# Casts, differences and sums held in the text's order, and background loads begun a turn earlier, in a hybrid HGRN2/GLA decoder trunk

## The chip, the cores and the metric

The kernel runs on one core of one Trainium2 chip, as one launch. The metric is the device time of that launch in microseconds (us); smaller is better. The core has a matmul engine (TensorE, PE in the profile; its weight loads are PEld), VectorE (DVE), ScalarE (ACT), GpSimd (POOL) and SyncE (SP). Each engine works off its own queue in order and waits on semaphores for the others. DMA transfers are issued here from SP's queue (loads) and POOL's queue (mostly stores).

## What is computed

The reference is one layer of a conditioned decoder trunk on a sequence of 1024 positions with 1024 channels, in float32. The normalised and modulated input `h` goes through one wide projection `w_in`; its columns feed eight HGRN2 heads and four GLA heads, gates and merge gates. Cut to what matters:

```python
h = rms_norm(x, norm_w) * (1 + scale) + shift
hq, hf, hi, hz, gq, gk, gv, gz, ga, mg = split(h @ w_in)
# HGRN2: f = lb + (1-lb)*sigmoid(hf); log_f = log f; k = (1-lb)*sigmoid(-hf); q = silu(hq); v = hi
# GLA:   log_a = log_sigmoid(ga @ alpha_w + alpha_b) / 16;  q, k, v = gq, gk, gv
# each head, in chunks of 64:  S_t = diag(decay_t) S_{t-1} + k_t v_t^T,  o_t = S_t^T q_t
y_h = rms_norm(o_hgrn) * silu(hz);  y_g = rms_norm(o_gla) * silu(gz)
u_h, u_g = y_h @ w_branch[0], y_g @ w_branch[1]
merged = sigmoid(mg[0]) * u_h + sigmoid(mg[1]) * u_g
out = rms_norm(x + gate * (merged @ w_out), final_norm_w)
```

## The kernel before

**Matmuls in three passes.** Every large product is done in a faster float format (fp32r): an operand is split into a high part, which is a cast on ACT (L202 in `split`, L208 in `pinned_split`), and a low part, the operand minus the high part, on DVE (L203, L209). PE then adds three products: high by high, high by low, low by high. So before PE can use a loaded weight block, a load, a cast on ACT and a subtraction on DVE must have been done.

**Jobs.** Matmul work is a list of jobs that the class `Stream` goes through. A job `Feat` projects 128 features of one head (L591: 8 steps, called units here, of 6 matmuls, into a PSUM tile `pd`). A job `Vjob` is a part of the value projections (L1864), which are done as two-by-two block products with seven instead of eight products (the Strassen-Winograd scheme); these need differences of blocks of `h` (`make_factor`, L1703, stored to memory as `fx`) and sums of blocks of the weights (`v_sums`, L1718 to L1724, stored as `vs`; L1824 to L1828 in `Vjob.prep` for the first value projection). The job list is: the value projection of the GLA heads, the projections of the GLA heads, the value projection of the HGRN heads, and the three projections of each of the eight HGRN heads. The later stages (merge gates, both branch projections, output) use the same scheme (L1315), and their weight sums are made in advance in `weight_sums` and stored as `ws`.

**What sets the order.** The Python text issues all instructions in one sequence. `Stream.ahead` issues the loads (`load_feat`, L573) and splits (`split_feat`) of later jobs while a job runs. After each unit `weave` lets two side tracks advance: `side`, where a head's attention runs beside the projections of the next (`attention`, L641 to L816), and `back`, the background: `alpha_side` (the decays of the last two GLA heads, L920 to L939), then `v_sums`, then `prepare`, which calls `weight_sums` for 16 blocks, then `gate_side`. Only the first generator of a track runs. Each `yield n` says how many units of the main stream are to pass before the generator goes on, and the number in `stream.back.append` how many to wait at the start.

Over this text lies the framework's scheduler. It keeps dependences, but may place an instruction on its engine's queue ahead of those that stand before it in the text, or behind them, by its own estimate of when inputs are ready and by priorities. `tc.keep_in_program_order` takes an instruction out of that: it keeps the text's place on its engine. Before, it is used only for the casts in `pinned_split`. The sums of `weight_sums` have a lowered priority (`BEHIND = -400`), by which they fill gaps.

**Attention of a head**, as far as it matters: ACT and DVE scale q and k (L641 to L654), PE makes scores in several block sizes (L649, L680, L738 to L749) with evictions between them, DVE masks the last ones (L753), ACT copies the score blocks into the tile `scT` (L758, L761 and the four of L764), PE transposes k (L775), ACT evicts that (L776), and PE makes the chunk states (L795) and then the outputs (L814, L816). For an HGRN head the gates are made just before from a projection: L1070 and L1071 on ACT, L1072 to L1074 on DVE.

**Memory.** Nearly all tiles are one of 46 slots of 4 KB per partition. A slot that is used again makes its new writer wait for the last reader, and for a store out of it.

## Time and profile before

| | us |
|---|---|
| median of 3 runs (lowest to highest) | 1217.03 (1217.02 to 1219.02) |
| profiled execution, own time | 1218.36 |
| its span, first to last instruction | 1216.7 |
| mean granted PE clock | 0.988 |

PE is busy for 96% of the span, DVE for 70%, ACT for 48%, POOL for 10%; the DMA engines move 181 GB/s on the mean. The profile names an instruction by its line, the engine, the operation and the tiles (output <- inputs; `b` is any slot). A number in square brackets behind a row is the idle time of its engine just before it, and what ended it. Busy time of PE is modelled, so idle time of PE that ends with a named release is the safer number. The granted clock is what the throttle let PE have, with 1.00 for full speed.

### The profile page before, as it was taken

The numbers are of one execution on the slowest core, as the hardware profiler recorded it, in microseconds if no ns is written. First come the engines' busy times: TensorE is split into PE (matmuls) and PEld (weight loads), VectorE is DVE, ScalarE is ACT, GpSimd is POOL, SyncE is SP. The second block draws the span as 40 slices with busy tenths as digits, with TensorE's granted clock in tenths as the row PEclk, the third lists the DMA queues.
The fourth block names the chain that finished last, engine by engine and source line by source line (L and its number), as shares of the span: only waits on it lengthen the run. The fifth ranks groups of instructions, "written<-read, shape, count | busy, mean of one in ns | idle before, by whom it ended". The sixth has DMA issues, their size and how long they took to land.

```text
span 1216.7 us, 20300 instructions
## 1 busy us (share of the span) xinstructions
PE 1173.9 (96%) x8137; PEld 956.0 (79%) x8137; DVE 846.7 (70%) x1270; ACT 584.0 (48%) x859; POOL 122.9 (10%) x256
## 2 busy tenths in 40 slices
PE   7998999999999999899998999999999999999997
PEld 6775777788878788688886888878878888878886
DVE  4746567668565966777875896786454765988994
ACT  5674365643353744244234245356644544544554
POOL 4211101011100123011111000000020000000000
PEclk9998999999999999899998999999999999999999
DMA  9756336384644669345545542245697846435433
GB/s 325 258 212 227 111 121 191 114 283 140 225 129 166 226 225 327 106 147 192 173 155 160 165 119 79 83 140 162 219 325 278 265 157 212 147 104 173 160 102 137
DMA packets 150353, 220.19 MB, mean 181 GB/s; under 512 B 8939, under 2 KB 107297, under 8 KB 150258
## 3 DMA queue, kind: packets, MB, share of 16 engines
q1 hardware_dynamic: 131970, 157.84, 41.6%
q0 software_dynamic: 18240, 61.04, 13.1%
q8 instruction: 64, 1.05, 0.4%
q14 instruction: 31, 0.25, 0.1%
q10 hardware_dynamic: 48, 0.01, 0.0%
HBM read 153.84 MB, written 65.01 MB: 180 GB/s over the span
## 4 chain that ended last, share of the span: by engine, by line
PE 48%; issue 35%; DMA 5%; DVE 4%; POOL 4%; ACT 2%; SPq 1%; POOLq 0%; DVEq 0%; ACTq 0%
PE pd L1315 10%; PE pd L591 8%; PE pd L1864 8%; PE pm L1315 5%; PE sc_ps L1315 5%; PE pd L1492 3%; DMA b<-in_ada_w_dram 2%; POOL ws L1173 2%; PE pd L383 2%; PE sc_ps L1492 2%; PE pm L1492 1%; DVE b L209 1%; PE pm L814 1%; PE sc_ps L383 1%; PE pm L816 1%
## 5 line engine op out<-in xcount | busy, mean ns | idle before, releaser
L591 PE MATMUL pd<-b,b 128*128 128x512 f32 x1632 | 393.8, 397 | 0.0
L591 PEld LDWEIGHTS pd<-b,b 128*128 128x128 f32 x1632 | 304.8, 190 | 65.2 <-issue 0.7
L1315 PE MATMUL pd<-b,b 128*128 128x512 f32 x720 | 173.0, 391 | 1.5 <-DVE b L1302 1.0
L1864 PE MATMUL pd<-b,b 128*128 128x512 f32 x672 | 164.1, 398 | 3.0 <-ACT b L1747 1.7
L1315 PEld LDWEIGHTS pd<-b,b 128*128 128x128 f32 x720 | 134.0, 188 | 31.8 <-DVE b L1302 1.5
L1864 PEld LDWEIGHTS pd<-b,b 128*128 128x128 f32 x672 | 123.8, 188 | 36.9 <-ACT b L1747 4.9
L1258 DVE TENSOR_TENSOR b<-b,b 128x1024 fp32r<-128x1024 f32 x56 | 68.3, 1223 | 69.8 <-ACT b L1257 56.9
L202 ACT CAST b<-b 128x1024 fp32r<-128x1024 f32 (+1 forms) x70 | 65.9, 951 | 80.0 <-DMA b<-in_w_in_dram 22.9
L203 DVE TENSOR_TENSOR b<-b,b 128x1024 fp32r<-128x1024 f32 (+1 forms) x70 | 76.7, 1101 | 36.7 <-ACT b L202 35.8
L1257 ACT CAST b<-b 128x1024 fp32r<-128x1024 f32 x56 | 58.4, 1049 | 66.3 <-PE pm L1315 17.6
L1315 PE MATMUL sc_ps<-b,b 128*128 128x512 f32 x324 | 78.7, 391 | 0.6 <-ACT b L1287 0.6
L209 DVE TENSOR_TENSOR b<-b,b 128x1024 fp32r<-128x1024 f32 x44 | 52.7, 1225 | 35.8 <-ACT b L208 34.2
L1315 PE MATMUL pm<-b,b 128*128 128x512 f32 x300 | 72.1, 389 | 0.0
L1315 PEld LDWEIGHTS sc_ps<-b,b 128*128 128x128 f32 x324 | 60.5, 188 | 14.1 <-ACT b L1287 1.3
L1235 DVE TENSOR_TENSOR b<-b,b 128x1024 fp32r<-128x1024 f32 x48 | 57.8, 1222 | 19.7 <-ACT b L1234 13.9
L1234 ACT CAST b<-b 128x1024 fp32r<-128x1024 f32 x48 | 49.7, 1049 | 44.9 <-PE pd L1315 15.5
L1315 PEld LDWEIGHTS pm<-b,b 128*128 128x128 f32 x300 | 56.3, 188 | 11.7
L700 ACT COPY xb<-b 128x512 f32<-128x512 f32 x48 | 29.2, 619 | 62.4 <-PE sc_ps L680 36.4
L383 PE MATMUL pd<-b,b 128*128 128x512 f32 x192 | 52.8, 408 | 6.0 <-DVE b L359 5.2
L1173 POOL DMA_DIRECT2D ws<-b x64 | 34.5, 540 | 187.2 <-DVE b L1167 67.1
L383 PEld LDWEIGHTS pd<-b,b 128*128 128x128 f32 x192 | 34.8, 190 | 18.7 <-DVE b L359 6.1
L208 ACT CAST b<-b 128x1024 fp32r<-128x1024 f32 x44 | 44.3, 1050 | 6.8 <-PE pd L1864 3.5
(315 smaller groups left out, 1720.1 us busy)
## 6 DMA issues: line engine op xcount, KB each, us to landing
b<-in_w_in_dram SPq DMA_DIRECT2D x72, 512.0 KB, 4.9
ws<-b POOLq DMA_DIRECT2D x64, 256.0 KB, 4.4
b<-ws SPq DMA_DIRECT2D x32, 512.0 KB, 4.3
b<-in_x_dram SPq DMA_DIRECT2D x16, 512.0 KB, 6.2
b<-in_ada_w_dram SPq DMA_DIRECT2D x32, 256.0 KB, 6.5
v<-b POOLq DMA_DIRECT2D x32, 256.0 KB, 3.1
b<-v SPq DMA_DIRECT2D x16, 512.0 KB, 5.0
b<-fx SPq DMA_DIRECT2D x16, 512.0 KB, 4.2
```

What stands on the lines that cost most here:

```text
L202: nc.scalar.copy(hi, src)
L203: nc.vector.tensor_sub(lo, src, hi.bitcast(F32))
L209: nc.vector.tensor_sub(lo, src, hi.bitcast(F32))
L383: nc.tensor.matmul(accs[f], wg(a, d, f), b[d][:, half * 512:half * 512 + 512], start=(d == 0 and n == 0), stop=(d == KT - 1 and n == 2))
L591: nc.tensor.matmul(ps[0:w, th * 512:(th + 1) * 512], a[:, k, 0:w], b[:, th * 512:(th + 1) * 512], start=(k == 0 and n == 0), stop=(k == KT ...
L1173: nc.gpsimd.dma_start(w_sums[b][i // 2][q][:, i % 2 * 512:i % 2 * 512 + 512], parts[p].rearrange("p k f -> p (k f)"))
L1235: nc.vector.tensor_sub(lo, src, hi.bitcast(F32))
L1257: nc.scalar.copy(hi, t)
L1258: nc.vector.tensor_sub(lo, t, hi.bitcast(F32))
L1315: nc.tensor.matmul(o, a[:, sl], c, start=(p in (1, 5) and kt == 0 and n == 0), stop=(kt == 3 and n == 2), skip_group_check=True)
L1492: nc.tensor.matmul(o, a, b, start=(p in (1, 5) and kt == 0 and n == 0), stop=(kt == 3 and n == 2), skip_group_check=True)
L1864: nc.tensor.matmul(st.bank[i], x_, w_, start=(p in (1, 5) and kk == 0 and a == 0 and n == 0), stop=(kk == 1 and a == 1 and n == 2), skip_g ...
```

## The change

Five edits, all of them about order and time of issue; the arithmetic is the same.

- `split_feat` uses `pinned_split`, so the casts of all projection weights are held in the text's order on ACT.
- Held on DVE: the subtractions of `make_factor`, the sums of the value weights in `Vjob.prep` and `v_sums`, and the sums of `weight_sums`, which lose their lowered priority.
- `prepare` issues the loads of block n before the sums of block n − 1, so that a block's loads are a whole turn ahead of its sums; the waits between steps and the slot threshold (12 to 11) are adapted. In `v_sums` the wait between loads and sums is 9 units, not 6.
- In `attention` the four copies L764 move behind the eviction L776 of the transposed k.
- `alpha_side` for the last two GLA heads starts after 72 units, not 62.

```diff
-    def pinned_split(src):
-        hi, lo = S.get([2, 512], F32R), S.get([2, 512], F32R)
-        tc.keep_in_program_order(nc.scalar.copy(hi, src))
+    held = tc.keep_in_program_order
+
+    def pinned_split(src, hi=None, lo=None):
+        if hi is None:
+            hi, lo = (S.get(list(src.shape[1:]), F32R) for _ in range(2))
+        held(nc.scalar.copy(hi, src))
         nc.vector.tensor_sub(lo, src, hi.bitcast(F32))
         return hi, lo
...
-        split(raw[:, :, 0:w], hi[:, :, 0:w], lo[:, :, 0:w])
+        pinned_split(raw[:, :, 0:w], hi[:, :, 0:w], lo[:, :, 0:w])
...
-        for j in range(4):
-            nc.scalar.copy(scT[32 * j:32 * j + 32, :, 32 * j:32 * j + 32], blk[32 * j:32 * j + 32])
         scoring.discard(me)
         yield 3
...
         S.free(k)
+        for j in range(4):
+            nc.scalar.copy(scT[32 * j:32 * j + 32, :, 32 * j:32 * j + 32], blk[32 * j:32 * j + 32])
         yield 2.5
...
-    def weight_sums(b, i):
+    def load_blocks(b, i):
         src = sources[b][i]
-        while len(S.free_list) < 12 or paused[0]:
-            yield 1
-        x1, x2 = S.get([4, 2, P]), S.get([4, 2, P])
...
-        yield 6
+        return x
+
+    def weight_sums(b, i, x1, x2):
...
-        with tc.high_priority(offset=BEHIND):
-            add(parts[7], x1[:, :, 0], x1[:, :, 1])
-            add(parts[5], x1[:, :, 1], x2[:, :, 1])
-        yield 1.5
-        with tc.high_priority(offset=BEHIND):
-            add(parts[6], parts[7], x2[:, :, 1])
-            add(parts[3], parts[6], x2[:, :, 0])
+        held(add(parts[7], x1[:, :, 0], x1[:, :, 1]))
+        yield 1
+        held(add(parts[5], x1[:, :, 1], x2[:, :, 1]))
+        yield 1
+        held(add(parts[6], parts[7], x2[:, :, 1]))
+        yield 1
+        held(add(parts[3], parts[6], x2[:, :, 0]))
...
     def prepare():
-        for b in range(4):
-            for i in range(4):
-                yield from weight_sums(b, i)
+        todo = [(b, i) for b in range(4) for i in range(4)]
+        blocks_of = {}
+        for n in range(len(todo) + 1):
+            while n < len(todo) and (len(S.free_list) < 11 or paused[0]):
+                yield 1
+            if n < len(todo):
+                blocks_of[n] = load_blocks(*todo[n])
+            if n:
+                yield from weight_sums(*todo[n - 1], *blocks_of.pop(n - 1))
+            yield 7
...
-        nc.vector.tensor_sub(xq[dst][kk], xq[x][kk], xq[y][kk])
+        held(nc.vector.tensor_sub(xq[dst][kk], xq[x][kk], xq[y][kk]))
...
-            yield 6
+            yield 9
...
-                add(wq[0, 0][kk], wq[0, 0][kk], wq[0, 1][kk])
-                add(wq[0, 1][kk], wq[0, 1][kk], wq[1, 1][kk])
+                held(add(wq[0, 0][kk], wq[0, 0][kk], wq[0, 1][kk]))
+                held(add(wq[0, 1][kk], wq[0, 1][kk], wq[1, 1][kk]))
...
-        stream.back.append([alpha_side((2, 3)), 62, 1, 0])
+        stream.back.append([alpha_side((2, 3)), 72, 1, 0])
```

The order on the engines is shown at three places. Line numbers of the changed kernel are a little higher: L202/L203 and L208/L209 are both L211/L212 there, L641 to L657 are 3 higher, L764 is L780, L776 is L777, L900 to L1074 are 3 higher, L1703 is L1712.

Place 1, DVE's queue before the first GLA head (near 100 us). L1703/L1712 are the subtractions of `make_factor`, L900 to L906 (L903 to L909) the chain of the first decays, L359/L362 an eviction of q and k projections. Before:

```order
L203 TENSOR_TENSOR b_154<-b_973,b_146 128x512
L1703 TENSOR_TENSOR b_630<-b_630,b_915 128x1024
L1703 TENSOR_TENSOR b_834<-b_834,b_973 128x1024
L1703 TENSOR_TENSOR b_915<-b_915,b_1124 128x1024
L1703 TENSOR_TENSOR b_973<-b_973,b_1125 128x1024
L900 TENSOR_SCALAR b_1046<-b_1045 128x1024
L901 SCALAR_TENSOR_TENSOR b_1045<-b_1046,b_1045 128x1024
L906 TENSOR_TENSOR b_1046<-b_1046,b_1045 128x1024
L209 TENSOR_TENSOR b_1076<-b_1031,b_1075 128x1024
L359 TENSOR_SCALAR b_1089<-pd_173 128x512
```

Now:

```order
L203 TENSOR_TENSOR b_154<-b_973,b_146 128x512
L903 TENSOR_SCALAR b_1046<-b_1045 128x1024
L904 SCALAR_TENSOR_TENSOR b_1045<-b_1046,b_1045 128x1024
L909 TENSOR_TENSOR b_1046<-b_1046,b_1045 128x1024
L212 TENSOR_TENSOR b_1076<-b_1031,b_1075 128x1024
L362 TENSOR_SCALAR b_1089<-pd_173 128x512
L364 COPY b_1115<-sc_ps 128x512
L362 TENSOR_SCALAR b_1095<-pd_173 128x512
L212 TENSOR_TENSOR b_1165<-b_1035,b_1164 128x1024
L364 COPY b_1121<-sc_ps 128x512
L362 TENSOR_SCALAR b_1101<-pd_174 128x512
L1712 TENSOR_TENSOR b_1125<-b_834,b_1125 128x1024
```

The subtractions of `make_factor` left the stretch ahead of the decay chain and stand behind the third eviction; the second L212 now stands ahead of that one.

Place 3, ACT's queue at the first HGRN head (near 480 us). L641/L644 starts the scaling of q, L1070/L1073 and L1071/L1074 make the gates of the head, L202/L211 are casts of projection weights. Before:

```order
L946 ACTIVATE b_4065<-pd_3962 128x1024
L641 COPY xb<-b_4065 128x32x32
L202 CAST b_4486<-b_4263 128x1024
L202 CAST b_4609<-b_4385 128x1024
L1070 ACTIVATE b_4139<-pd_4068 128x1024
L1071 ACTIVATE b_4140<-pd_4068 128x1024
```

Now, and behind it DVE's queue at the same head (L1075 to L1077 are the gates on DVE, L1168 to L1174 sums of `weight_sums`, L645 to L648 the scaling that ends before PE's first scores):

```order
L949 ACTIVATE b_4031<-pd_3934 128x1024
L211 CAST b_4069<-b_3818 128x1024
L644 COPY xb<-b_4031 128x32x32
L1073 ACTIVATE b_4101<-pd_4034 128x1024
L1074 ACTIVATE b_4102<-pd_4034 128x1024
L211 CAST b_4144<-b_3856 128x1024
```

```order
L1077 TENSOR_SCALAR b_4102<-b_4102,oml 128x1024
L1168 TENSOR_TENSOR b_4122<-b_4015 128x512
L1170 TENSOR_TENSOR b_4121<-b_4015,b_4016 128x512
L1172 TENSOR_TENSOR b_4121<-b_4122,b_4016 128x512
L212 TENSOR_TENSOR b_4145<-b_3856,b_4144 128x1024
L1174 TENSOR_TENSOR b_4122<-b_4121,b_4016 128x512
L645 TENSOR_TENSOR xb<-b_4031,b_4101 128x32x8
L646 TENSOR_TENSOR xb<-b_4031,b_4101 128x32x8x2
L654 TENSOR_TENSOR b_4031<-b_4031,b_4101 128x256
L647 TENSOR_TENSOR xb<-xb,b_4101 128x32x16
L648 TENSOR_TENSOR xb<-xb,b_4101 128x32x8
```

On ACT no cast stands between L644 and L1073 any more; on DVE four sums and a subtraction stand between L1077 and L645.

Place 4, ACT's queue at a later HGRN head (near 654 us). L758/L761, L761/L764 and L764/L780 copy score blocks, L776/L777 evicts the transposed k. Before:

```order
L946 ACTIVATE b_5700<-pd_5579 128x1024
L202 CAST b_6370<-b_6138 128x1024
L202 CAST b_6245<-b_6022 128x1024
L641 COPY xb<-b_5700 128x32x32
L758 COPY scT<-sc_ps 32x4x32 x4
L761 COPY scT<-sc_ps 64x4x64 x2
L764 COPY scT<-blk 32x8x32 x4
L776 COPY b_5804<-pm_5805 128x512
```

Now:

```order
L949 ACTIVATE b_5672<-pd_5551 128x1024
L644 COPY xb<-b_5672 128x32x32
L761 COPY scT<-sc_ps 32x4x32 x4
L764 COPY scT<-sc_ps 64x4x64 x2
L211 CAST b_5775<-b_5549 128x1024
L777 COPY b_5779<-pm_5780 128x512
L777 COPY b_5779<-pm_5786 128x384
L780 COPY scT<-blk 32x8x32 x4
```

The two casts left the place ahead of L641; another cast, for the next job, stands ahead of the evictions of the transposed k, and the four copies stand behind them.

More of the change, by code (lines that the diff above doesn't have):

```diff
@@ L27 @@
 N_SLOTS = 46
-EVICT_FIRST, BEHIND = 300, -400
+EVICT_FIRST = 300
 PACE, PACE_H = 1.08, 1.15
@@ L1151, in hybrid_trunk_kernel @@
     paused = [False]
-    def weight_sums(b, i):
+    def load_blocks(b, i):
         src = sources[b][i]
-        while len(S.free_list) < 12 or paused[0]:
-            yield 1
-        x1, x2 = S.get([4, 2, P]), S.get([4, 2, P])
-        for kh, x in enumerate((x1, x2)):
-            nc.sync.dma_start(x.rearrange("p k a f -> p k (a f)"),
+        x = [S.get([4, 2, P]) for _ in range(2)]
+        for kh in range(2):
+            nc.sync.dma_start(x[kh].rearrange("p k a f -> p k (a f)"),
                               src[kh * 512:(kh + 1) * 512, :].rearrange("(k p) f -> p k f", p=P))
-        yield 6
+        return x
+    def weight_sums(b, i, x1, x2):
         s1, s2 = S.get([2, 4, P]), S.get([2, 4, P])
```

11 lines of the change are left out of this document (5 added, 6 removed).

## The prediction

> **What bounds the kernel now.** I read the busy shares first, then TensorE's (PE's) waits, then the granted clock in stretches of 20 us, and last the timelines of the long stalls. From the page, the engine row and the group of the weight casts (busy and mean ns, idle before it):
>
> ```profile
> PE 1173.9 (96%) x8137; PEld 956.0 (79%) x8137; DVE 846.7 (70%) x1270; ACT 584.0 (48%) x859; POOL 122.9 (10%) x256
> ```
>
> ```profile
> L202 ACT CAST b<-b 128x1024 fp32r<-128x1024 f32 (+1 forms) x70 | 65.9, 951 | 80.0 <-DMA b<-in_w_in_dram 22.9
> ```
>
> Matmuls bound the kernel, and no work is taken from PE, so the change can only win what PE idles or runs at a lower clock. ACT is half idle, but 80.0 us of its idle time stand in front of one line, the cast of a projection weight; where such a cast is early in ACT's queue and its data late, all behind it waits. PE's own waits (total, times, longest):
>
> ```profile
> PE pm L795 <- ACT b L776: 9.2, 5, 5.2
> PE pd L383 <- DVE b L359: 5.2, 1, 5.2
> PE sc_ps L649 <- DVE xb L645: 4.8, 1, 4.8
> PE pm L775 <- ACT b L922: 2.7, 1, 2.7
> PE pd L1864 <- ACT b L1747: 1.7, 4, 1.1
> ```
>
> Four single stalls make 17.9 us (5.2, 5.2, 4.8, 2.7), and four more before L795 share 9.2 − 5.2 = 4.0. The stretches (columns PE, PEld, DVE, ACT, POOL busy, granted clock, DMA share, GB/s) show a second price:
>
> ```profile
> 100.00:120.00 20.00, 14.77 (x51) 10.66 (x50) 10.87 (x12) 8.95 (x10) 3.27 (x7) 0.83 0.61 241
> 220.00:240.00 20.00, 19.14 (x96) 16.56 (x97) 10.58 (x16) 13.97 (x15) 0.00 (x0) 0.91 0.28 84
> 460.00:480.00 20.00, 20.00 (x89) 16.52 (x88) 12.71 (x22) 10.36 (x10) 5.20 (x10) 1.00 1.03 333
> 480.00:500.00 20.00, 15.19 (x114) 12.38 (x113) 16.41 (x26) 5.23 (x7) 3.42 (x7) 0.84 0.61 209
> 520.00:540.00 20.00, 19.13 (x106) 16.28 (x105) 16.02 (x28) 10.54 (x19) 2.69 (x5) 1.00 0.57 173
> 640.00:660.00 20.00, 14.94 (x174) 11.95 (x172) 10.45 (x19) 10.21 (x19) 2.16 (x4) 0.94 0.52 155
> 660.00:680.00 20.00, 19.83 (x126) 17.26 (x130) 15.40 (x26) 3.63 (x6) 2.70 (x5) 0.89 0.64 203
> ```
>
> The clock is full where PE is never idle (460) and where it idles for 0.9 us (520, one of the small L795 waits), and drops after each of the four long stalls: 20 × (1 − 0.83) = 3.4 us lost, then 1.8, 3.2, and 20 × (0.06 + 0.11) = 3.4: 11.8 us together. The four stalls thus cost about 30 us, and everything hangs on what holds them.
>
> **The change, place by place.** It adds and removes no instruction (DVE has 1235 rows in the order before and after); it moves them, so each term is a stall that goes or comes.
>
> *Place 1, about 107 us: subtractions held behind L359.*
>
> ```profile
> 99.53 0.69 ACT L898 ACTIVATE b<-pm,vec 128x512 f32<-128x512 f32 x1 [0.17 <-PE pm L897]
> 103.35 1.23 DVE L1703 TENSOR_TENSOR b<-b,b 128x1024 f32<-128x1024 f32 x1 [4.14 <-DMA h<-b]
> 104.50 0.69 DVE L900 TENSOR_SCALAR b<-b 128x1024 f32<-128x1024 f32 x1
> 106.86 1.02 PE L920 MATMUL pm<-b,b 128*128 128x512 f32 x2
> 112.37 0.69 DVE L359 TENSOR_SCALAR b<-pd 128x512 f32<-128x512 f32 x1
> 113.11 1.65 PE L383 MATMUL pd<-b,b 128*128 128x512 f32 x3 [5.23 <-DVE b L359]
> 113.36 1.98 ACT L208 CAST b<-b 128x1024 fp32r<-128x1024 f32 x2
> ```
>
> L900 could have begun at 100.2, when L898 ended; it began at 104.50 since VectorE (DVE) stood at an L1703 that was placed early and waited 4.14 for a store. In the new order no L1703 stands before the first L359, so L900 to L359 move up by 4.3 us and PE restarts at 108.8. About 2 us of stall are left (PE then arrives at 106.86, where the L920 stood). Against this, two L359s now stand behind an L209 whose cast is the second of the row at 113.36, and one behind an L1703 too (1.23): by the same shift they come 0.7 and 0.6 late, 1.3 us. The two L920s of this place are paid later (0.5 us; the first had lain in the stall). Clock: 3.4 more if the 2 us leave it full, nothing if not. Ends 4.3 − 0.5 = 3.8 and 4.3 + 3.4 − 1.3 − 0.5 = 5.9; I take 5.
>
> *Place 2, 217.8 us: the alpha chain starts 10 units later.*
>
> ```profile
> 218.45 1.64 ACT L764 COPY scT<-blk 32x256 f32<-32x256 f32 x4
> 220.12 0.69 ACT L922 ACTIVATE b<-pm,vec 128x512 f32<-128x512 f32 x1
> 220.82 1.28 ACT L946 ACT_TABLE_LOAD   x1
> 220.86 0.90 PE L775 MATMUL pm<-ident,b 128*128 128x128 f32 x3 [2.75 <-ACT b L922]
> ```
>
> L775 needed the bank that L922 had to empty, and L922 stood behind four L764s. Both causes go: the L920s come some 25 us later, and the L764s move behind L776. That is 2.75 + 1.8 = 4.5. But the chain's table loads and activations (1.28 each, and 1.0 as L946's kind) now stand among the evictions and root casts of the next head, which PE waits for there. One table load with its activation delays a cast by up to 2.3, in two places 4.6 and at worst a clock window (1.8) more; with slack nothing. I take 2.4, so a net gain of 2 (−2 to 4.5).
>
> *Place 3, 489 us: casts held, but sums held too.*
>
> ```profile
> 479.78 9.68 PE L591 MATMUL pd<-b,b 128*128 128x512 f32 x42
> 480.60 1.29 DVE L1170 TENSOR_TENSOR b<-b,b 128x512 f32<-128x512 f32 x2
> 484.18 2.00 ACT L202 CAST b<-b 128x1024 fp32r<-128x1024 f32 x2 [5.75 <-DMA yg<-b]
> 486.08 1.01 ACT L1070 ACTIVATE b<-pd 128x1024 f32<-128x1024 f32 x1
> 487.01 1.22 DVE L203 TENSOR_TENSOR b<-b,b 128x1024 fp32r<-128x1024 f32 x1
> 493.49 0.64 DVE L645 TENSOR_TENSOR xb<-xb,b 128x256 f32<-128x256 f32 x1
> 494.27 2.36 PE L649 MATMUL sc_ps<-xb,b 128*32 128x80 f32 x64 [4.81 <-DVE xb L645]
> ```
>
> L1070 could have started when PE began the next job at 479.8, but two casts for later jobs stood ahead of it and waited 5.75. From L1070's start to L645's end it is 494.13 − 486.08 = 8.05, against 9.68 of PE's work. In the new order L1070 follows L641 at once, which alone would end L645 at 487.9, before PE asks at 489.46. Yet DVE now holds four sums (0.65 each, the row at 480.60) and an L203 (1.22) inside this chain: 3.8 us, so 491.7 and a stall of 2.2. The gain is 494.1 − 491.7 = 2.4, and 5.6 if the clock stays full (+3.2); if DVE gets the sums done while it waits for L1070 anyway, 8.0. I take 4.2. In the other heads the later value products (L814, L816) give PE work in between, and the held sums cost nothing there; if that cover is gone, each head pays like this one.
>
> *Place 4, 654.6 us: casts held.*
>
> ```profile
> 650.27 0.29 DVE L753 COPY_PREDICATED blk<-mask,sc_ps 128x128 f32<-128x128 int32 x1
> 651.94 3.01 PE L591 MATMUL pd<-b,b 128*128 128x512 f32 x12
> 653.31 2.00 ACT L202 CAST b<-b 128x1024 fp32r<-128x1024 f32 x2 [7.25 <-DMA ws<-b]
> 656.15 1.05 ACT L758 COPY scT<-sc_ps 32x128 f32<-32x128 f32 x4
> 657.22 0.74 ACT L761 COPY scT<-sc_ps 64x256 f32<-64x256 f32 x2
> 657.87 1.64 ACT L764 COPY scT<-blk 32x256 f32<-32x256 f32 x4
> 659.53 0.97 ACT L776 COPY b<-pm 128x512 f32<-128x512 f32 x2
> ```
>
> Without the two casts L758 starts when the scores are masked, at L753's end, 650.6. L758, L761, one held cast (1.05) and L776 take 3.8, so 654.4, and PE asks at 654.95. The whole 5.2 + 3.4 = 8.6 should go, with half a us to spare; a cast that comes 2.5 us late costs 2, which leaves 6.6. I take 8.3.
>
> *The other four L795 waits* (4.0): the L764s leave the chain (−1.64) and a held cast enters it (+1.0), 0.6 each: 2 us, between 0 and 4. *The L1864 waits near 385 us*: casts that stood ahead of two evictions now stand behind them, about 1.4 new for 1.7 old; 0, ±1.5. One activation load of the third GLA head waits for a store: −0.5.
>
> *The held sums of the value weights* (L1824 to L1827 and those of `v_sums`) stay ahead of the same L209 subtractions: 0; out of place, one costs its 1.22. *The loads a whole turn ahead* hold two more of 46 slots but move no matmul; from the last head on, the orders agree, so nothing after 900 us changes.
>
> **Sum:** 5 + 2 + 4.2 + 8.3 + 2 − 0.5 = 21.0, against the profiled execution's 1218.36 (span 1216.7): 1197.4. The median of the runs, 1217.03, is 1.3 lower: **1196 us**.
>
> The Trainium skill (TensorE: Matmul & The Clock Gate, Part 1: The HAM clock gate) says that the clock halves only after an idle window of about 3.4 us, which runs free of the work. By it the stalls of 2 us left at places 1 and 3 would cost no clock, and the sum would be about 2 better (0.9 and 1.4). The trace agrees only in part: the 2.75 us of L775 were enough for 0.91.
>
> The Trainium skill (ScalarE: Activation LUTs, What ACT_TABLE_LOAD costs) gives a switch of tables 1.28 us and a drain of 1.38. With the drain, place 2 would lose 2.8 more with two loads (an estimate from that page). The trace agrees with the first number (1.28), and the load at 220.82 followed L922 without a gap.
>
> **The rivals.** (a) *Nothing new appears*: held sums and alpha chain all find slack. For it: DVE idles 30%. Places 1 to 4 at their best, 5.9 + 4.5 + 8.0 + 8.6, and 4.0: 31 us, 1186. (b) *The held sums and the moved chain bring new stalls, each with its clock window*: 3.8 + (−2) + 2.4 + 6.6 + 0, less 1.5 at 385 and 2 in the GLA heads: 7 us, 1210. Against it: the small L795 waits in this trace leave the clock full (the stretch at 520). (c) *Slower: a held cast waits for its load with ACT's queue behind it.* Each HGRN head now has a cast between L761 and L776. A load that lands after the cast's turn makes the whole chain to L795 late; the load burst at 460 (share 1.03) shows the queues full. The 22.9 us that ACT waits for weights would fall on PE, and at the 1.8 of L775 for four of eight heads 7 more: −21 + 30 = +9, 1226. It decides where loads, issued two jobs (some 20 us) ahead, land later than half a job before PE needs them. Against it, the page's median from issue to landing:
>
> ```profile
> b<-in_w_in_dram SPq DMA_DIRECT2D x72, 512.0 KB, 4.9
> ```
> (d) *The change doesn't do what it says*: the casts wait because a slot comes free late, and held, they wait as long elsewhere: the time stays, 1217.
>
> **How the numbers follow.** Forecast 0.47 (its own range 1190 to 1203), (a) 0.18, (b) 0.16, (c) 0.11, (d) 0.08. From 1184 to 1213 it holds the first three, 0.81. About 0.2% (2.4 us) is what can be told from no change: faster 0.84 (with a little of (d)), same 0.05, slower 0.11.
>
> **What would show it.** Right: the waits L383 (5.2 to 2), L649 (to about 2) and L795 (to under 3) shrink, L775 is gone, and the stretches at 480 and 640 to 680 are at clock 1.00. Wrong: casts L202 idle as long before them, L795 waits in most HGRN heads, or an alpha table load stands before PE's root matmuls with over 2 us.

## The result, and the profile after

The changed kernel takes 1203.0 us (median) against 1217.0 before: a ratio of 0.9877 with a 95% interval of 0.9858 to 0.9897, so 12 to 17 us faster. One of its four executions took 4095.9 us, which nothing here explains; it is left out of the ratio but not of the median, which is 1202.5 without it. The forecast was 1196 us, in a range from 1184 to 1213. The direction and the four places were right; of the 21 us expected, 14 came in the median and 16.7 in the profiled execution (1201.68 us, span 1200.0, against 1218.36 and 1216.7). Line numbers here are those of the changed kernel where a row of it is shown (L591 is L594 there, L1864 is L1873, L795 is L798, L649 is L652, L1315 is L1324). A clock window, below, is a stretch of 3.4 or 6.8 us in which the granted clock is 0.50.

Busy shares and the two groups of casts, from the page and the list of groups of the changed kernel:

```profile
PE 1167.3 (97%) x8137; PEld 949.7 (79%) x8137; DVE 845.9 (70%) x1270; ACT 583.3 (49%) x859; POOL 123.0 (10%) x256
...
L211 ACT CAST b<-b 128x1024 fp32r<-128x1024 f32 x78 | 79.7, 1047 | 11.0 <-PE pd L1873 4.1
...
L202 ACT CAST b<-b 128x1024 fp32r<-128x1024 f32 (+1 forms) x36 | 30.2, 859 | 15.6 <-DMA b<-wo 5.5 <-DVE b L992 2.2 <-DVE b L1106 2.1
```

The work is the same. The groups are cut differently now: of the 70 casts that L202 had, 34 are held and stand in L211 with the 44 of L208; the other 36, casts of other operands, stayed in L202. ACT's idle time in front of all 114 fell from 86.8 us (80.0 and 6.8) to 26.6 (11.0 and 15.6). PE's waits (total, times, longest):

```profile
PE pd L1873 <- DVE b L1784: 3.1, 2, 1.9
...
PE pd L386 <- DVE b L362: 2.1, 2, 1.9
PE pd L594 <- DVE b L212: 2.1, 1, 2.1
PE pm L817 <- DVE b L804: 2.0, 2, 1.6
...
PE pm L962 <- DVE b L203: 0.8, 1, 0.8
PE sc_ps L652 <- DVE xb L648: 0.7, 1, 0.7
...
PE pm L798 <- ACT b L777: 0.5, 1, 0.5
```

The four long stalls of before are gone or small: L795/L798 from 9.2 to 0.5, L383/L386 from 5.2 to 2.1, L649/L652 from 4.8 to 0.7, L775 from 2.7 to none in this list. But, apart from the start-up (left out here), the top is new: evictions of the value projection (L1784), weights (L212) and chunk states (L804), all on DVE. The stretches show the same, with the clock:

```profile
0.00:20.00 20.00, 14.06 (x66) 12.36 (x67) 7.73 (x21) 10.22 (x20) 13.80 (x56) 1.00 0.94 302
100.00:120.00 20.00, 17.41 (x72) 12.93 (x71) 14.05 (x16) 9.71 (x11) 4.33 (x9) 1.00 0.47 168
180.00:200.00 20.00, 17.69 (x191) 13.55 (x192) 16.29 (x31) 4.46 (x8) 3.79 (x8) 1.00 0.61 197
640.00:660.00 20.00, 20.00 (x126) 17.05 (x128) 17.34 (x28) 7.14 (x12) 3.79 (x7) 1.00 0.69 221
700.00:720.00 20.00, 18.20 (x198) 14.39 (x196) 19.22 (x36) 6.32 (x9) 1.08 (x2) 1.00 0.51 164
720.00:740.00 20.00, 18.11 (x200) 15.15 (x201) 16.07 (x25) 9.20 (x17) 1.62 (x3) 1.00 0.63 216
```

The clock reads 1.00 in all of them, and 640 to 660 has no idle time left. PE now idles in 180 to 200 and in 700 to 740, where it did not before. The 1.00 of the first row cannot be right, though. The same six small matmuls, in the changed kernel and in the kernel before, whose clock was full at that moment:

```profile
14.69 1.49 PE L231 MATMUL sc_ps<-ident,ones 128*128 128x128 f32 x6
```

```profile
14.73 0.83 PE L228 MATMUL sc_ps<-ident,ones 128*128 128x128 f32 x6
```

The clock record of the changed kernel begins only at 20 us, and the pace of its matmuls up to there is that of half clock.

Where the 16.7 us of the profiled execution came from can be followed by the start of the same matmul in both traces (before minus after, at points of time of the kernel before; the eight passes of the alpha chain's matmuls, 3.65 us, run later in the changed kernel and are taken out of the middle rows):

```
place                                   gain us   forecast
start-up, to 24 us                        -0.9       0
1: 107 us                                 +4.3      +5
value projection, 179 to 184 us           -3.1       0
2: 218 us (+4.3), 251 us (-1.0)           +3.3      +2
third GLA head, 302 us                    -0.6      -0.5
value projection, 386 to 402 us           -1.6       0
3: 489 us                                 +6.9      +4.2
four small L795 waits (three to 610 us)   +4.0      +2
4: 655 us                                 +7.4      +8.3
718, 736, 772 us and near them            -4.2       0
885 us                                    +1.2       0
sum                                       16.7      21.0
```

So the places that were forecast gave 4 us more than forecast, and three places that the forecast held at nothing took 9: that the sum is nearer to the forecast than its terms is partly luck. The other 2.7 us, from 16.7 to 14.0, are the distance of the two profiled executions from their medians (+1.3 and −1.3). The start-up is no part of that gain: the profiled execution of the changed kernel ran it at half clock and was 0.9 us late by 24 us.

### The profile page after: what moved, and what is told of

Read it like the earlier page. It is cut to its first block, busy times and chain, and to the rows that moved or that the text cites. A ratio compares the mean times of both kernels' runs of the same rounds, so it can differ in the third digit from the quotient of the medians.

```text
span 1200.0 us, 20302 instructions
## 1 busy us (share of the span) xinstructions
PE 1167.3 (97%) x8137; PEld 949.7 (79%) x8137; DVE 845.9 (70%) x1270; ACT 583.3 (49%) x859; POOL 123.0 (10%) x256
## 4 chain that ended last, share of the span: by engine, by line
issue 48%; PE 37%; POOL 7%; DMA 3%; DVE 3%; ACT 2%; SPq 0%; POOLq 0%; DVEq 0%; ACTq 0%
PE pd L1324 11%; PE sc_ps L1324 6%; PE pm L1324 6%; PE pd L1501 3%; POOL ws L1176 3%; PE pd L594 3%; PE pd L1873 2%; PE sc_ps L1501 2%; PE pm L1501 1%; POOL v L1763 1%; DMA b<-in_ada_w_dram 1%; DMA b<-in_x_dram 1%; POOL yh L889 1%; PE pm L817 1%; POOL qk L365 1%
## 5 line engine op out<-in xcount | busy, mean ns | idle before, releaser
L594 PE MATMUL pd<-b,b 128*128 128x512 f32 x1632 | 391.1, 395 | 2.1 <-DVE b L212 2.1
L594 PEld LDWEIGHTS pd<-b,b 128*128 128x128 f32 x1632 | 302.0, 188 | 67.1 <-DVE b L212 2.5
L1324 PE MATMUL pd<-b,b 128*128 128x512 f32 x720 | 173.1, 392 | 0.6 <-DVE b L1416 0.4
L1873 PE MATMUL pd<-b,b 128*128 128x512 f32 x672 | 163.6, 397 | 7.5 <-DVE b L1784 3.1
L1324 PEld LDWEIGHTS pd<-b,b 128*128 128x128 f32 x720 | 133.9, 188 | 31.0 <-DVE b L1416 0.9
L1873 PEld LDWEIGHTS pd<-b,b 128*128 128x128 f32 x672 | 123.0, 188 | 41.4 <-ACT b L1756 2.8
L212 DVE TENSOR_TENSOR b<-b,b 128x1024 fp32r<-128x1024 f32 x78 | 94.3, 1222 | 48.5 <-ACT b L211 47.6
L1267 DVE TENSOR_TENSOR b<-b,b 128x1024 fp32r<-128x1024 f32 x56 | 68.2, 1222 | 69.4 <-ACT b L1266 57.4
L1266 ACT CAST b<-b 128x1024 fp32r<-128x1024 f32 x56 | 58.4, 1050 | 66.1 <-PE pm L1324 17.6
L211 ACT CAST b<-b 128x1024 fp32r<-128x1024 f32 x78 | 79.7, 1047 | 11.0 <-PE pd L1873 4.1
L1324 PE MATMUL sc_ps<-b,b 128*128 128x512 f32 x324 | 78.7, 391 | 0.4 <-ACT b L1296 0.4
L1324 PE MATMUL pm<-b,b 128*128 128x512 f32 x300 | 72.1, 389 | 0.0
L1324 PEld LDWEIGHTS sc_ps<-b,b 128*128 128x128 f32 x324 | 60.5, 188 | 14.0 <-ACT b L1296 1.1
L1244 DVE TENSOR_TENSOR b<-b,b 128x1024 fp32r<-128x1024 f32 x48 | 57.7, 1219 | 18.6 <-ACT b L1243 12.1
L1243 ACT CAST b<-b 128x1024 fp32r<-128x1024 f32 x48 | 49.7, 1049 | 40.4 <-PE pd L1324 16.0
L1324 PEld LDWEIGHTS pm<-b,b 128*128 128x128 f32 x300 | 56.3, 188 | 11.7
L386 PE MATMUL pd<-b,b 128*128 128x512 f32 x192 | 52.3, 405 | 2.9 <-DVE b L362 2.1
L203 DVE TENSOR_TENSOR b<-b,b 128x1024 fp32r<-128x1024 f32 (+1 forms) x36 | 35.1, 983 | 28.2 <-ACT b L202 28.1
L817 PE MATMUL pm<-scT,b 128*128 128x128 f32 x256 | 47.0, 275 | 2.0 <-DVE b L804 2.0
L386 PEld LDWEIGHTS pd<-b,b 128*128 128x128 f32 x192 | 34.4, 188 | 15.4 <-DVE b L362 2.9
```

Source lines behind the costliest of these rows:

```text
L211: held(nc.scalar.copy(hi, src))
L212: nc.vector.tensor_sub(lo, src, hi.bitcast(F32))
L386: nc.tensor.matmul(accs[f], wg(a, d, f), b[d][:, half * 512:half * 512 + 512], start=(d == 0 and n == 0), stop=(d == KT - 1 and n == 2))
L594: nc.tensor.matmul(ps[0:w, th * 512:(th + 1) * 512], a[:, k, 0:w], b[:, th * 512:(th + 1) * 512], start=(k == 0 and n == 0), stop=(k == KT ...
L817: nc.tensor.matmul(o, vch(ch)[:, vh * P:(vh + 1) * P], scT[:, ch, :], start=True, stop=(ch == 0))
L1244: nc.vector.tensor_sub(lo, src, hi.bitcast(F32))
```

## Experiments

All runs are against the kernel before on the same chip; ratios with 95% intervals. Line numbers differ by a few from run to run: the eviction of the transposed k is L774, L777 or L779, the value projection L1867, L1873 or L1875.

**One part alone: the held casts.** Edit, on the kernel before:

```diff
+    def pinned_split(src, hi=None, lo=None):
+        if hi is None:
+            hi, lo = (S.get(list(src.shape[1:]), F32R) for _ in range(2))
+        held(nc.scalar.copy(hi, src))
...
-        split(raw[:, :, 0:w], hi[:, :, 0:w], lo[:, :, 0:w])
+        pinned_split(raw[:, :, 0:w], hi[:, :, 0:w], lo[:, :, 0:w])
```

> The kernel before with one part alone: the casts of the projection weights held in the text's order. If casts that were placed too early are what stops ACT at 484 and 654 us, the two long stalls there go with their clock windows: 4.8 + 3.2 and 5.2 + 3.4, about 16 us, less some 0.5 to 1 us in each of the other heads, where a held cast now stands between the score copies and the eviction of the transposed k: 1203 to 1206. ACT's idle time before these casts falls from 80 us to under 30. Rival: the casts wait for their data or a free slot wherever they stand; then ACT's idle time before them stays near 80 us and the time near 1217.

Measured: 1211.4 us, 0.9946 (0.9931 to 0.9961). The largest of PE's waits, from its list, and the group of the casts, from the page:

```profile
PE pm L798 <- ACT b L779: 9.5, 7, 2.2
```

```profile
L211 ACT CAST b<-b 128x1024 fp32r<-128x1024 f32 x78 | 79.8, 1048 | 8.0 <-PE pd L1867 4.5
```

The rival falls: ACT's idle time in front of the held casts is 8.0 us, and with the 36 that stayed in L202 (24.7) it is 32.7 where it was 86.8. So the casts had waited because they stood too early, and the waits at 484 and 654 us are gone (the longest before L798 is 2.2, and there is none before L652). But the gain is 5.6 us, not the 11 to 14 of the range: behind the held cast between the score copies and the eviction of the transposed k, PE waits 9.5 us in seven heads, 5.5 more than the four small waits there had been. Two of these waits, 2.2 us at 514 us and 2.1 at 607, are each followed by a clock window that the kernel before did not have. I had allowed 0.5 to 1 us a head and no window.

**One part alone: the moved copies.** The four copies L764 of `attention` go behind the eviction L776, as in the change.

```diff
-        for j in range(4):
-            nc.scalar.copy(scT[32 * j:32 * j + 32, :, 32 * j:32 * j + 32], blk[32 * j:32 * j + 32])
         scoring.discard(me)
...
         S.free(k)
+        for j in range(4):
+            nc.scalar.copy(scT[32 * j:32 * j + 32, :, 32 * j:32 * j + 32], blk[32 * j:32 * j + 32])
         yield 2.5
```

> The kernel before with one part alone: the four score copies behind the eviction of the transposed k. If they lengthen the chain to the chunk states, the four small waits there (4.0 us together) go, the stalls at 217 and 654 us each shrink by about 1.6: 1209 to 1212. Rival: the copies only trade places with work that is late next (the outputs need them): the time stays within 2 us of 1217.

Measured: 1211.1 us, 0.9946 (0.9928 to 0.9964), as expected. PE's list of waits has one wait before L795 left:

```profile
PE pm L795 <- ACT b L774: 3.4, 1, 3.4
...
PE pm L773 <- ACT b L922: 2.5, 1, 2.5
```

The four small ones are gone and the long one is 1.8 shorter (5.2 to 3.4), about the 1.64 of the copies. The wait for L922 is nearly as before (2.7 to 2.5): it was not the copies that made it.

**Both together.** The two edits above.

> The kernel before with two parts: the casts of the projection weights held, and the four score copies behind the eviction of the transposed k. Alone these gave 5.6 and 5.9 us. If they only add up: 1205.5. If they need each other (a held cast between the score copies and the eviction makes seven waits before the chunk states of 9.5 us in all, which the moved copies give room for), the stalls at 484 and 654 us and all these waits go together: 1200 to 1203.

Measured: 1201.9 us, 0.9877 (0.9851 to 0.9904). That is 15.5 us, where the two alone give 11.5. The interval holds the mere sum too (0.9892), so it is the waits that show that the casts need the copies moved: those before L798 fall from 9.5 to 2.0. And it is the time of the whole change (0.9877). All other parts of the change together therefore bring nothing on balance that these intervals could show, though the place at 107 us is still as before in this kernel:

```profile
PE pd L386 <- DVE b L362: 4.9, 1, 4.9
...
PE pm L798 <- ACT b L777: 2.0, 4, 0.6
```

The wait for L922 shrank to 0.5 here without a later alpha chain (PE's start at 219 us), and to 0.8 with the casts alone, so at place 2, too, the early casts had been the cause, not the chain's start.

**One part alone: the held subtractions of `make_factor`.**

```diff
-        nc.vector.tensor_sub(xq[dst][kk], xq[x][kk], xq[y][kk])
+        held(nc.vector.tensor_sub(xq[dst][kk], xq[x][kk], xq[y][kk]))
```

> The kernel before with one part alone: the subtractions of make_factor held on DVE. If they alone cause the wait at 107 us, it falls from 5.2 to about 2 with its clock window (-6). If holding them is also what makes the stall of 3.1 us at 179 to 184 us that only the changed kernel has (a held subtraction comes 15 us later, its slot is freed later, and the q load of the first GLA head behind it on SP's queue is late), that stall appears here too: 1213 to 1215 in all. Rival: the stall at 179 us comes from the later alpha chain or the held weight casts; then it is absent here and the time is 1210 to 1212.

Measured: 1216.6 us, 0.9986 (0.9971 to 1.0002), no clear change, and outside both ranges. From its list of waits:

```profile
PE pd L1867 <- DVE b L1778: 1.6, 1, 1.6
...
PE pd L386 <- DVE b L362: 1.1, 1, 1.1
```

The wait at 107 us falls to 1.1, and the place wins 6.3 us, as expected. The new wait for the value projection's eviction is there too (1.6), so that much of the 3.1 comes with this part, and not with the casts, the sums or the alpha chain. What was not expected is that the rest is lost later: the wait of 2.7 before L775 turned into one of 3.4 before L798 at 222 us, and one of 1.6 at 395 us is followed by a clock window.

**The change, with the subtractions for the products 6 and 4 not held.**

```diff
-        held(nc.vector.tensor_sub(xq[dst][kk], xq[x][kk], xq[y][kk]))
+        sub_ = nc.vector.tensor_sub(xq[dst][kk], xq[x][kk], xq[y][kk])
+        if p in (5, 7):
+            held(sub_)
```

> The changed kernel with the subtractions for the products 6 and 4 left to the scheduler, those for 5 and 7 held as in the change. If the held subtraction for product 6 is what makes the q load and with it DVE's evictions late, the waits for the eviction at 179 to 184 us (3.1 us) go or fall under 1 us, while the wait at 107 us stays near 2: about 1200, 2 to 3 us under the changed kernel's 1203. Rival: the q load is late because PE is 5 us earlier while transfers are not; then the waits stay and so does the time.

Measured: 1201.4 us, 0.9866 (0.9852 to 0.9881).

```profile
PE pd L1875 <- DVE b L1786: 0.6, 1, 0.6
```

The wait for the eviction falls from 3.1 to 0.6 and the one at 107 us stays. The time is 1.6 us less, within the intervals; the wait itself settles it. The chain can be read in the changed kernel's timeline (us, duration, engine, operation):

```profile
165.08 1.22 DVE L1712 TENSOR_TENSOR b<-b,b 128x1024 f32<-128x1024 f32 x1
166.33 3.78 SPq L1009 DMA_DIRECT2D b<-qk  x2
175.71 1.05 ACT L644 COPY xb<-b 128x1024 f32<-128x1024 f32 x1 [3.73 <-DMA b<-qk]
176.83 2.94 ACT L211 CAST b<-b 128x1024 fp32r<-128x1024 f32 x3
177.92 2.36 DVE L212 TENSOR_TENSOR b<-b,b 128x1024 fp32r<-128x1024 f32 x2 [2.30 <-ACT b L211]
180.19 0.68 DVE L1784 TENSOR_TENSOR b<-pd,b 128x512 f32<-128x512 f32 x1
180.93 1.88 PE L1873 MATMUL pd<-b,b 128*128 128x512 f32 x7 [1.89 <-DVE b L1784]
```

and before, from the same view of the kernel before:

```profile
147.62 1.23 DVE L1703 TENSOR_TENSOR b<-b,b 128x1024 f32<-128x1024 f32 x1
158.80 0.32 SPq L1006 DMA_DIRECT2D b<-qk  x1
```

The subtraction for product 6 came at 147.6 when it was free, and comes at 165.1 when held. A slot that it reads is taken next by the load of q and k for the first GLA head, which is issued at 166.3 in place of 158.8; in the run here, where that subtraction is free again, at 154.5. ACT stands for 3.73 us at L644, which scales that q, with three casts behind it; DVE's L212 waits for the casts, the eviction L1784 stands behind L212, and PE behind that.

**The change, with the weight sums of before.**

```diff
-        held(add(parts[7], x1[:, :, 0], x1[:, :, 1]))
...
+        with tc.high_priority(offset=-400):
+            add(parts[7], x1[:, :, 0], x1[:, :, 1])
+            add(parts[5], x1[:, :, 1], x2[:, :, 1])
...
     def prepare():
...
+        for b in range(4):
+            for i in range(4):
+                yield from weight_sums(b, i)
```

> The changed kernel with the weight sums of before: loads just ahead of their sums, sums as gap fillers with lowered priority. If the later, held sums are what fills DVE to 100% between 690 and 760 us, the stalls of 2.1 and 1.6 us at 718 and 736 us go: 1198 to 1200. Rival: the earlier loads and the held order are needed, since sums that wait for their loads hold DVE: stalls return elsewhere in the HGRN heads and the time is 1206 or more.

Measured: 1203.4 us, 0.9884 (0.9854 to 0.9914): neither. Both halves of the two theories are seen; the largest wait of the HGRN heads is:

```profile
PE sc_ps L652 <- DVE xb L648: 3.8, 1, 3.8
```

No wait of over 0.6 us is left between 700 and 780 us, so the new sums are part of those. But at 486 us a sum that was placed early and waited 3.6 us for its load makes PE wait 3.8. The new sums take that away and give about the same back later. This holds with the later start of the alpha chain, which this version has: with held casts, the sums of before and the chain at 62 units, PE waits only 0.3 there (the version with casts and copies, above).

**The change without most of the gate's accumulation.** Seven of the eight products of the gate's modulation are left out.

```diff
             else:
-                nc.vector.scalar_tensor_tensor(gacc, b, cs[:, k:k + 1], gacc, ALU.mult, ALU.add)
+                pass
```

> The changed kernel without seven of the eight accumulations of the gate's modulation on DVE (left out: products 2 to 8 of that sum; their loads stay). If the gate's 7 x 1.28 us meeting the late sums is what makes the stalls at 718 and 736 us, these shrink from 3.7 to under 1 us together and the time to about 1200. Rival: the sums alone do it; then the stalls stay above 3 us and the time at 1203.

Measured: 1198.7 us, 0.9841 (0.9821 to 0.9862), as expected. The wait before L594 falls to 0.4 and the one before L817 goes. The stretches:

```profile
700.00:720.00 20.00, 19.60 (x204) 15.52 (x202) 19.56 (x39) 6.32 (x9) 1.94 (x4) 1.00 0.63 192
720.00:740.00 20.00, 20.00 (x219) 17.30 (x218) 12.96 (x22) 11.23 (x20) 1.82 (x4) 1.00 0.61 203
```

PE's busy time there rises from 18.20 and 18.11 to 19.60 and 20.00. So the 3.7 us at 718 and 736 need both: the sums, which end later than before (the last store at 723 us, 666 before), and the gate's 9 us, which come behind them in the background. The rows of the changed kernel show how they meet:

```profile
715.29 1.05 ACT L211 CAST b<-b 128x1024 fp32r<-128x1024 f32 x1
715.78 1.28 DVE L1047 SCALAR_TENSOR_TENSOR b<-b,cs,b 128x1024 f32<-128x1024 f32 x1
718.39 0.69 DVE L1168 TENSOR_TENSOR b<-b 128x512 f32<-128x512 f32 x1
719.00 1.22 DVE L212 TENSOR_TENSOR b<-b,b 128x1024 fp32r<-128x1024 f32 x1
720.27 2.14 PE L594 MATMUL pd<-b,b 128*128 128x512 f32 x8 [2.07 <-DVE b L212]
...
738.20 0.68 PE L817 MATMUL pm<-scT,b 128*128 128x128 f32 x4 [1.62 <-DVE b L804]
```

The cast was done at 716.3; DVE came to its L212 at 719.0, since L1047, the head's own work and a sum (L1168) stood before it.

**Sums that do not wait for room.** In the change, the sums of block n − 1 stand behind the loads of block n, and these wait for 11 free slots and through the pause of the loads. Here, on the version with 5 and 7 held:

```diff
-        for n in range(len(todo) + 1):
-            while n < len(todo) and (len(S.free_list) < 11 or paused[0]):
-                yield 1
...
+        while done < len(todo):
+            room = n < len(todo) and len(S.free_list) >= 11 and not paused[0]
+            if not room and n == done:
+                yield 1
+                continue
+            if room:
+                blocks_of[n] = load_blocks(*todo[n])
+                n += 1
+            if n - done > 1 or not room:
+                yield from weight_sums(*todo[done], *blocks_of.pop(done))
+                done += 1
+            yield 7
```

> The changed kernel with the subtractions for the products 6 and 4 not held (1201.4 so far) and, in addition, sums that no longer wait for room for the next block's loads. If the sums come later than needed because the first one waits through the pause of the loads (first store of a sum at 444 us, 285 us before), sums and gate side move ahead and the stalls at 718 and 736 us (3.4 us) change: 1197 to 1200. Rival: only the first block moves, DVE is as full in the heads from 690 us on, and the time stays at 1201 to 1202.

Measured: 1199.1 us, 0.9846 (0.9827 to 0.9866), in the expected range, but not for the expected reason: the waits at 714 and 732 us are still 1.9 and 1.0 us. Of the 2.5 us that its profiled execution is ahead of the version before it, 1.4 are there by 116 us, in the start-up and in the clock at 107 us, ahead of any sum. Most of the rest, 1.3, is won at 386 to 402 us, where four waits for held casts and their subtractions (2.2 us in the version before it) are gone. The versions with held casts and the sums and loads of before do not have these four either, so this part may well be the edit's, at a place where I had not looked for it; it is not shown by an experiment of its own.

**The gate ahead of the sums.** On that version, the order of the two background generators exchanged:

```diff
+        stream.back.append([gate_side(), 4, 1, 0])
         stream.back.append([prepare(), 4, 1, 0])
-        stream.back.append([gate_side(), 4, 1, 0])
```

> The version with sums that do not wait for room (1199.1), and the gate's accumulations ahead of the weight sums in the background, so near 330 us in place of 710 to 735 us. If the gate's 9 us on DVE at 100% are what makes the stalls at 714 and 732 us (2.9 us), they go: 1195 to 1197. Rival: the sums, now 20 us later, fill that place; then the stalls stay and the time is 1199 or more.

Measured: 1200.1 us, 0.9851 (0.9831 to 0.9871), above the range. The waits at 714 and 732 us are gone, as expected, and the time is not better, since the gate's work makes a wait where it now stands:

```profile
336.64 1.28 DVE L1047 SCALAR_TENSOR_TENSOR b<-b,cs,b 128x1024 f32<-128x1024 f32 x1 [4.25 <-DMA b<-in_ada_w_dram]
...
343.36 0.89 PE L683 MATMUL sc_ps<-xb,b 128*32 128x48 f32 x45 [3.79 <-DVE blk L666]
```

An accumulation that the scheduler placed ahead waits 4.25 us for its load with a head's work behind it: the fault that the change takes away at the other places, at one that it does not hold.

**The alpha chain after 62 units again.**

```diff
-        stream.back.append([alpha_side((2, 3)), 72, 1, 0])
+        stream.back.append([alpha_side((2, 3)), 62, 1, 0])
```

> The changed kernel with the alpha chain started after 62 units again. If the later chain is what spares the wait of 2.75 us with its clock window at 218 us, 4 us come back there and 0.8 at 251 us go: 1205 to 1207. Rival: with held casts and moved copies ACT reaches the chain's evictions in time anyway (a wait of 0.5 at 219 us in the version with those two parts): 1202 to 1203.5, within 0.5 us of the changed kernel, unless the sums, which move up with it, change the stalls at 718 and 736 us.

Measured: 1196.5 us, 0.9821 (0.9802 to 0.9841), 6.5 us better than the change, with intervals that do not meet, and better than either theory had it. No wait at 218 us comes back, and none is left at 251. The rest of the gain lies at 179 us and in the late heads, because the whole background moves up: the first store of a sum is at 310 us (444 in the change), the last at 699 (723), and the gate's seven accumulations begin at 701 (712). The wait for weights near 717 us is 1.1 in place of 2.1, and no wait for L804 is in the list (2.0 in the change). The later start of the chain was a loss.

**A version that beats both.** The kernel before with the held casts, the moved copies and the subtractions held for products 5 and 7; sums, loads and alpha chain as before.

```diff
+        held(nc.scalar.copy(hi, src))
...
+        pinned_split(raw[:, :, 0:w], hi[:, :, 0:w], lo[:, :, 0:w])
...
+        sub_ = nc.vector.tensor_sub(xq[dst][kk], xq[x][kk], xq[y][kk])
+        if p in (5, 7):
+            held(sub_)
```

> The kernel before with the held casts, the moved copies, and the subtractions for the products 5 and 7 held (weight sums, loads and alpha chain as before). With the casts and copies alone: 1201.9, of which the profiled execution still had 4.9 us at 107 us and a clock window of 6.8 us at half speed behind it. If the three are the whole benefit and the other parts are not needed: the wait at 107 us falls to 1.9, 3 to 6 us less, 1196 to 1199, at or under every version with the new sums. Rival: the new sums are needed once DVE's early stretch is shorter; then waits come back in the HGRN heads and the time stays above 1200.

Measured: 1194.3 us, 0.9803 (0.9785 to 0.9822): 23.7 us under the kernel before on that chip (1218.0), under the expected range, and its interval does not meet that of the change. Two of its waits:

```profile
PE pm L798 <- ACT b L777: 1.9, 4, 0.6
...
PE pd L386 <- DVE b L362: 1.1, 1, 1.1
```

The wait at 107 us is 1.1, less than the 1.9 expected, since with the earlier start PE does two passes of the alpha chain just before it. The version above (1196.5), which has the new sums and loads as well, is not told apart from this one; nothing here shows a gain from them.

With the gate ahead of the sums in this version:

> Held casts, moved copies, held subtractions for 5 and 7, and the gate's accumulations ahead of the weight sums. In the kernel before, the gate's accumulations stood at 687 to 706 us with no wait of PE near them. If place is all that counts, nothing changes against the same version with the gate last: within 1 us. Rival: the sums come 20 us later and meet the last heads: 1 to 3 us slower.

Measured: 1196.1 us, 0.9818 (0.9791 to 0.9845). It lies 1.8 us above, as the rival had it, but with overlapping intervals, so no difference is shown. A wait of 1.9 us before L652 at 484 us is new in its profile.

## Why the prediction was right, and where its sum was off

**Place 1** (5 forecast, 4.3 measured). The chain moved up as worked out: PE restarts at 109.84 with 1.92 us of wait, forecast 108.8 and about 2. In the profiled execution the clock stayed at 1.00 there, and that was luck: the version with the products 5 and 7 held waits the same 1.92 us and loses about 1.8 more (last section).

**The clock's price before** (11.8 us read, about 9). I took every drop of the granted clock in the stretches for lost time. But half clock costs nothing while PE stands still, and each drop began inside the stall. At place 4, in the kernel before:

```profile
657.40:660.17 2.77, 0.00 (x1) 0.00 (x1) 0.69 (x1) 2.70 (x8) 0.54 (x1) 0.51 0.04 13
660.17:664.26 4.09, 4.09 (x17) 3.90 (x18) 1.28 (x4) 0.33 (x1) 0.00 (x0) 0.50 0.16 64
```

Only the 4.1 us after the stall cost anything, 2.0 us, not 3.4; reckoned so, the places 1 to 3 cost 2.5, 1.5 and 3.1.

**Place 1, what the held subtractions do elsewhere** (0 forecast, −3.1). The step that failed followed them only ahead of L359, to the evictions just behind. It did not ask which slot the later ones keep, and what SP's queue puts into that slot: the load of q and k. The run with these subtractions alone shows the first wait (1.6), and the one with only 5 and 7 held takes it away (0.6). The second, 1.2 at 184 us, appears only with the later alpha chain, whose matmuls PE did at that point before.

**Place 2** (2 forecast, 3.3 measured). The wait went with its clock window, and the moved chain cost 1.0, not 2.4. But the cause was read wrongly. I put the wait down to the L764s and to the start of the chain. Held casts leave 0.8 of it with the old start, with moved copies 0.5; copies alone leave 2.5. The term "the L920s come some 25 us later" bought nothing and cost 6.5 us in the whole.

**Place 3** (4.2 forecast, 6.9 measured). The size was off by one term: the 8.05 us from L1070 to L645 held a wait of its own. The row of L1070 at 486.08 is followed in the kernel before by:

```profile
488.74 0.81 DVE L1072 TENSOR_SCALAR b<-b,oml,lb 128x1024 f32<-128x1024 f32 x1
```

L1070 ended at 487.09 and L1072 came 1.65 later, behind sums and an L203 that I then added a second time. After the change:

```profile
478.54 1.03 ACT L1073 ACTIVATE b<-pd 128x1024 f32<-128x1024 f32 x1 [2.85 <-PE pd L594]
479.60 0.82 DVE L1075 TENSOR_SCALAR b<-b,oml,lb 128x1024 f32<-128x1024 f32 x1 [1.31 <-ACT b L1073]
...
487.93 0.64 DVE L648 TENSOR_TENSOR xb<-xb,b 128x256 f32<-128x256 f32 x1
...
488.72 0.51 PE L652 MATMUL sc_ps<-xb,b 128*32 128x80 f32 x17 [0.70 <-DVE xb L648]
```

From L1073 to the end of L648 it is 488.57 − 478.54 = 10.03; 8.05 − 1.65 + 3.8 would have been 10.2. The wait left is 0.7, not 2.2, and no clock window follows.

**Place 4** (8.3 forecast, 7.4 measured) and **the small L795 waits** (2 forecast, 4.0 measured) went as described, place 4 with the smaller price of the clock: 5.2 + 2.0 = 7.2. The experiments add what the working did not say: the casts need the copies moved. Held alone they make PE wait 9.5 us at seven such places.

**"… hold two more of 46 slots but move no matmul"** (the loads a whole turn ahead; 0 forecast, with 1.5 either way near 385 us, −1.6 measured at 386 to 402). Four waits for held casts and their subtractions, 2.1 us, stand there in every version whose sums wait for room, and in none of the others. Which slot or load links the two was not followed.

**"In the other heads … the held sums cost nothing there"** (0 forecast, −4.2 measured near 718 to 780 us). This is the step that cost most. I checked each sum against its own head and not where the background as a whole comes to stand. The first sum waits for the second block's loads, and these wait through the pause, so the first store of a sum is at 444 us (285 before) and the last at 723 (666). The gate's accumulation follows at 710 to 737 (687 to 708 before), in heads where DVE is then at 96% (19.22 of 20 us from 700 us on; 17.06 in the kernel before at the same work of PE, 720 to 740). A full DVE alone does no harm: from 700 to 720 it had 19.14 in the kernel before, and PE never idled. The price was what stood in DVE's queue ahead of the L212 and L804 that PE waited for. The run without seven of the eight accumulations wins 4.3 us, with an interval that just touches that of the change. And the held sums were not alone in this: with the alpha chain at 62 units the same sums cost about 2 us less in these heads.

**The rivals.** (c), casts that wait for their loads, did not come: 11.0 us in front of the held ones in all, none of it ended by a load. (d) did not, either. (b) comes nearest to what was measured, new stalls in several places, but without its clock windows in the profiled execution. What stays open is how much sums that do not wait for room gain, and what the loads a turn ahead are worth without the later start: the parts were not tried apart there.

## What to carry to other kernels

Where engines work in order, an instruction that waits for a transfer holds all behind it. Keep such instructions in the text's order on the engine that the bottleneck waits for, but follow each held one to what it delays, also through the slot it keeps and the load that takes the slot next. Do it part by part: here two parts, of which one needs the other, gave the whole gain, a third was good for two of its four products, and the rest took back as much as it gave. Background work is to be placed as a whole: a start 10 units later moved sums and gate ahead of work that PE waited for, and cost 6.5 us. And half clock is a price only while PE has work.

## What the runs showed of the hardware

The same wait of PE can cost a clock window or none. The changed kernel and the one with products 5 and 7 held both wait 1.92 us at the same matmul at 109.84 us. Their timelines, and the stretch of the second (the first is shown above, 1.00):

```profile
109.84 0.97 PE L386 MATMUL pd<-b,b 128*128 128x512 f32 x3 [1.92 <-DVE b L362]
```

```profile
109.85 1.40 PE L386 MATMUL pd<-b,b 128*128 128x512 f32 x3 [1.92 <-DVE b L362]
```

```profile
100.00:120.00 20.00, 17.75 (x69) 13.54 (x69) 13.39 (x15) 9.71 (x11) 4.20 (x8) 0.91 0.45 151
```

In the second the three matmuls after the wait take 1.40 us in place of 0.97, and the clock of the stretch is 0.91: about 1.8 us lost. What differs is where the wait falls. In the traces of all 14 kernels here every change of the granted clock lies on a grid of 3.413 us, within 0.002 us. In the second trace one step of that grid runs from 106.76 to 110.17 us and holds the whole wait; the step after it is at half clock. In the first an edge at 108.72 (worked out from the record's edges at 19.98 and 1197.58) cuts the wait into 0.80 and 1.12 us.

The other waits bear this out. Taken over all 14 traces, between 25 us and the end and with the clock full, 19 steps held 1.92 us or more of idle time of PE (by the modelled ends of its matmuls), and each was followed by half clock; 12 held from 1.5 to 1.88 us, and one of these was (1.55 us, the wait at 395 us with the held subtractions alone). What sets that one apart is open. The Trainium skill (TensorE: Matmul & The Clock Gate, Part 1: The HAM clock gate) says that its window runs free of the work, which agrees; that an idle window of about 3.4 us is needed does not, since 1.92 us within one step were enough here.
